# A scheduled GLA loop, one slot deeper, with an order of preference inside the slot

## The chip, the cores and the metric

The kernel runs on one NeuronCore of a Trainium2 chip. The metric is device time in microseconds (us) of one execution, the median of several runs. The engines are TensorE (PE, with its weight loads shown apart as PEld), VectorE (DVE), ScalarE (ACT), GpSimd (POOL) and SyncE (SP, which here only issues DMAs). Each engine takes its instructions in the order in which they stand in its queue.

## What is computed

One inference step of a two-layer backbone over 256 context tokens and 1024 latent tokens, width 1024. Layer 0 mixes tokens by gated linear attention (GLA) in both directions, layer 1 by softmax attention. Both have an adaptive norm in front, a SiLU gate and a residual. The change touches only the GLA layer:

```python
def step(S, inp):                       # per chunk, per head, per direction
    qi, ki, vi, gi = inp
    b = jnp.cumsum(gi, axis=2)
    qe = qi * jnp.exp(b)
    ke = ki * jnp.exp(-b)
    a = jnp.where(mask, jnp.einsum("bhtk,bhsk->bhts", qe, ke), 0.0)
    o = jnp.einsum("bhts,bhsv->bhtv", a, vi) + jnp.einsum("bhtk,bhkv->bhtv", qe, S)
    S = jnp.exp(b_last[:, :, 0, :])[..., None] * S + jnp.einsum(
        "bhsk,bhsv->bhkv", ki * jnp.exp(b_last - b), vi)
    return S, o
...
o = rms_norm(o_f + flip(o_b), onorm).reshape(B, T, GLA_VD).astype(h.dtype)
y = (o * jax.nn.silu(gate)) @ w_out
```

There are 4 heads, with keys of 128 and values of 256 columns. The outputs are both residual streams, the new scan states, and the keys and values of the context.

## The kernel before

Tokens lie in 10 tiles of 128. Products with large weights are made of three float16 products each (high by high, high by low, low by high), eight blocks deep, so one projection is 24 matmuls (`mm3`, line 129).

**The loop.** `gla` runs over heads 0 to 4 and, for each, over the 10 tiles: 50 slots. In a slot of head h it works on two heads at once. For head h it prepares a tile: `decay` makes the log decay (a product into the PSUM bank "z", then absolute value, exp and log on ACT, and a split in two float16 parts on DVE and POOL); `decayed` sums it along the chunk (bank "cs") and scales queries and keys with it (`en`, `qe`); `intra` transposes the scaled keys (bank "kt", line 617), copies them to SBUF (`ks`, DVE, line 619), makes the scores (line 623), masks them with a predicated copy (DVE, line 626) and adds both directions (`at`, POOL, line 628); `outer` makes keys times values (bank "U", lines 639 and 642), copies one direction away (`u`, ACT, line 644) and runs the first scan direction with the other (`Sa` on POOL, `Wa` on DVE, lines 662 and 666); `local` multiplies the scores with the values and the queries with the state into bank "A" (line 682) and ACT copies the result to `oa` (line 684). For head h-1 it finishes a tile: `combine` runs the other scan direction (`Sc`, `Wc`), multiplies it with the queries (bank "o", line 694), adds `oa` and takes the norm; `gated` multiplies with the gate `gx` (DVE, line 706) and writes the product to DRAM (`og_d`, a DMA on SP, line 707). `value_gate` projects values of head h and the gate of head h-1 in one product 512 wide (256 wide in head 0 and in the last pass); ACT takes the halves out of the bank (lines 558 and 562).

Beside these, slots carry pieces of the next head's query and key projections (`qk_piece`, 24 matmuls 512 wide, placed by the table `PIECES`), the conditioning of the next layer (`gemv`, `mod_sum`, `affine`), the loading and splitting of weights (`fill` and `split_ahead`: a maximum on DVE, its power of two over one small matmul in bank "o", `pow2`, then ACT and DVE for the two halves), and at the end the first tiles of the output projection.

**What sets the order.** A scheduler orders each engine's queue while the program is built: it takes the instruction of the lowest priority number that a model of the engines holds ready, and the number grows as the program is written down. In a slot the program is written as: `local` of the slot before, `decayed` of this slot, `decay` two slots ahead, `value_gate` of this slot, `intra`, `combine`, `gated`, fillers, `outer`. The loop has eight PSUM banks: two for "mm" (projections, taken in turn), one each for "z", "cs", "A", "kt", "U" and "o". The scores and the local product share "A". The gate `gx` has two SBUF buffers, `v` two.

Of the kernel before, what the change touches and what calls it, by code (L numbers as in the profile page):

```python
# [43 lines left out]

OUT = (1, 0, 2, 3, 4)

G_SCALE = 32.0
# [6 lines left out]
class K:  # L54
# [22 lines left out]

    def pow2(self, mx, n=1, cross=True):  # L80
# [208 lines left out]
    def gemv(self, l, b, to):  # L289
        nc = self.nc  # L290
        ps = self.bank("mm")
        for k in range(KT):
            j = k % 4
            nc.tensor.matmul(
                ps[32 * j : 32 * j + 32, 0:256], self.cst[:, k, :], to[:, k, :],
                start=k < 4, stop=k >= 4, tile_position=(0, 32 * j), skip_group_check=True,
            )
        m = self.t(self.ew, [P, 256], F32, "mod")
        nc.scalar.copy(m, ps[:, 0:256])
        return l, b, m  # L300
# [43 lines left out]
    def affine_rows(self, gb):  # L344
        ps = self.bank("mm")[0:32, 0:P]
        self.nc.tensor.transpose(ps, gb.rearrange("p s i k -> p (s i k)"), self.ident)
        r = self.t(self.ew, [P, 256], F32, "mod")[0:32, 0:P]
        self.nc.vector.tensor_copy(r, ps)
        self.nc.sync.dma_start(self.gb_d.rearrange("s i (k p) -> (s i k) p", p=P), r)
# [202 lines left out]
    def value_gate(self, h, i, w):  # L552
        a, b = 0 if h < GH else DV, 2 * DV if h > 0 else DV
        ps = self.bank("mm")
        self.tok_proj(i, [t[:, :, a:b] for t in w[0:2]], ps[:, a:b])
        if h < GH:
            v = self.t(self.tl, [P, DV], F32, "v", bufs=2)
            self.nc.scalar.activation(v, ps[:, 0:DV], AF.Copy, scale=self.inv_v[h])
            self.v[h][i] = v
        if h > 0:  # L560
            x = self.t(self.ew, [P, DV], F32, "gx")
            self.nc.scalar.activation(x, ps[:, DV:], AF.Copy, scale=self.inv_g[h - 1])  # L562
            self.silu(x, DV)
            return x
# [7 lines left out]
    def decay(self, h, i):  # L572
        nc = self.nc
        z = self.bank("z")[:, 0 : 2 * DK]
        nc.tensor.matmul(
            z.rearrange("p (d k) -> p d k", d=2), self.r[:, i * P : i * P + P],
            self.wa2[:, :, h * DK : h * DK + DK], start=True, stop=True,
        )
        u = self.t(self.ew, [P, 2 * DK], F32, "ls")
# [5 lines left out]
        nc.vector.scalar_tensor_tensor(g, u, G_SCALE, g, ALU.mult, ALU.add)  # L585
        hi = self.t(self.tl, [P, 2, DK], F16, "ghi", bufs=3)
        lo = self.t(self.tl, [P, 2, DK], F16, "glo", bufs=3)
        hf, lf = (t.rearrange("p d k -> p (d k)") for t in (hi, lo))
# [5 lines left out]
    def decayed(self, h, i, g):  # L594
        nc = self.nc
        cs = self.bank("cs")[:, 0:260].rearrange("p (d k) -> p d k", d=2)
        for d in range(2):
            for j in range(2):
                nc.tensor.matmul(cs[:, d, :], g[j][:, d, :], self.cum[:, d, :], start=j == 0, stop=j == 1)
        en = self.t(self.ew, [P, 2, P], F32, "en")  # L600
# [4 lines left out]
        self.mark = nc.vector.tensor_tensor(en, en, k.unsqueeze(1).to_broadcast([P, 2, P]), ALU.mult).ins  # L605
        qe = self.t(self.tl, [P, 2, P], F32, f"qe{i}")
        nc.vector.tensor_tensor(qe, ep[:, :, 0:P], q.unsqueeze(1).to_broadcast([P, 2, P]), ALU.mult)
        eb = self.t(self.tl, [P, 2, 2], F32, f"eb{i}")
        nc.gpsimd.tensor_copy(eb, ep[:, :, P : P + 2])
        return {"qe": qe, "ke": en, "eb": eb}  # L610

    def intra(self, i, st):
        nc = self.nc
        ke, qe = st["ke"], st["qe"]
        kt = self.bank("kt")[:, 0 : 2 * P].rearrange("p (d k) -> p d k", d=2)
        for d in range(2):
            nc.tensor.transpose(kt[:, d, :], ke[:, d, :], self.ident)
        ks = self.t(self.ew, [P, 2, P], F32, "ks")
        nc.vector.tensor_copy(ks, kt)
        ab = self.bank("A")  # L620
        ap, st["o"] = ab[:, 0 : 2 * P].rearrange("p (d k) -> p d k", d=2), ab[:, 2 * P :]
        for d in range(2):
            nc.tensor.matmul(ap[:, d, :], ke[:, d, :], qe[:, d, :], start=True, stop=True)
        am = self.am[self.ia % len(self.am)]
        self.ia += 1
        nc.vector.copy_predicated(am, self.mask, ap)
        at = self.t(self.tl, [P, P], F32, "at", bufs=2)
        nc.gpsimd.tensor_tensor(at, am[:, 0, :], am[:, 1, :], ALU.add)
        st["at"], st["ks"] = at, ks


    def outer(self, h, i, a, st, prev, last):
        nc = self.nc
        c = 1 - a
        ub = self.bank("U").rearrange("p (d k) -> p d k", d=2)
        v, ks = self.v[h][i], st["ks"]
        needa = i < NTP or not last
        if needa:
            nc.tensor.matmul(ub[:, a, :], ks[:, a, :], v, start=True, stop=True)
        st["u"] = None  # L640
        if i < NTP or prev is not None:
            nc.tensor.matmul(ub[:, c, :], ks[:, c, :], v, start=True, stop=True)
            st["u"] = self.t(self.tl, [P, DV], F32, f"u{i}")
            nc.scalar.copy(st["u"], ub[:, c, :])
        st["S"], st["W"] = self.scan(h, i, a, prev, ub[:, a, :] if needa else None, st["eb"], "a")
# [29 lines left out]
    def local(self, h, i, a, st):  # L675
        nc = self.nc
        o = st["o"]
        terms = [(st["at"], self.v[h][i])]
        if st["S"] is not None:
            terms.append((st["qe"][:, a, :], st["S"]))  # L680
        for j, (x, y) in enumerate(terms):
            nc.tensor.matmul(o, x, y, start=j == 0, stop=j == len(terms) - 1)
        st["oa"] = self.t(self.tl, [P, DV], F32, f"oa{i}")
        nc.scalar.copy(st["oa"], o)


    def combine(self, h, i, c, st, prev):
# [3 lines left out]
        if sc is not None:  # L691
            o = self.bank("o" if h < GH - 1 else ("o", "U", "z", "cs")[self.io % 4])[:, 0:DV]
            self.io += 1
            nc.tensor.matmul(o, st["qe"][:, c, :], sc, start=True, stop=True)
            og = self.t(self.ew, [P, DV], F32, "og", bufs=3)
# [37 lines left out]
    def gla(self, wq, w, filler):  # L733
        asc = list(range(NTP, NT)) + list(range(NTP))
        orders = [asc if h % 2 == 0 else asc[::-1] for h in range(GH + 1)]
        st = [[None] * NT for _ in range(GH)]
        g = {n: self.decay(0, asc[n]) for n in range(2)}
        local = None
        for h in range(GH + 1):
            order = orders[h]  # L740
            a, ends = (0, (NT - 1, NTP - 1)) if h % 2 == 0 else (1, (NTP, 0))
            starts = (NTP, 0) if h % 2 == 0 else (NT - 1, NTP - 1)
            if h < GH:
                self.inv_v[h] = self.mulcol(self.inv_h, w[2][0], self.gcp, f"inv_v{h % 2}")
            if h > 0:
                self.inv_g[h - 1] = self.mulcol(self.inv_h, w[2][1], self.gcp, f"inv_g{h % 2}")
            prev = cprev = None
            for n, i in enumerate(order):
                slot = h * NT + n
                if i in starts:  # L750
                    prev = cprev = None
                if local:
                    self.local(*local)
                    local = None
# [6 lines left out]
                if h < GH:  # L761
# [6 lines left out]
                with self.tc.issue_after(self.mark):  # L768
                    while self.jobs:
                        run(self.jobs.pop(0))  # L770
                filler(slot)
                if h < GH:
                    self.outer(h, i, a, s, prev, i in ends)
                    prev, local = s, (h, i, a, s)
                    if i < NTP and i in ends:
                        self.final_state(h, a, prev)
                if n == 4 and h < GH:
                    nw = self.nw = self.wtile((2, 1)[h % 2])
                    self.jobs.append(self.load_g(nw, h))
# [6 lines left out]
                if h == 1 and n == 3:  # L786
                    self.fold_qk(1, wq)
                if h < GH - 1:
                    for j, c in PIECES[h % 2].get(n, ()):
                        self.qk_piece(h + 1, j, c, wq)  # L790
            if h < GH:
                w = nw

# [514 lines left out]
def emit(ctx, tc, I, O, dbg=None, stop=None):  # L1308
# [29 lines left out]
    with ExitStack() as c:  # L1338
# [285 lines left out]
```

## Time and profile before

| | |
|---|---|
| three timed runs | 1301.16, 1304.89 and 1310.17 us, median 1304.89 |
| the profiled execution | its span from first to last instruction, 1302.5 us |
| PE, DVE, ACT, POOL busy | 1214.8, 923.3, 704.9, 360.3 us |
| mean granted PE clock | 0.983 of full speed |
| GLA loop on the time axis | about 76 to 600 us, the last slots mixed with the output projection |

How to read the profile: busy time is the time in which an engine had an instruction in it; a PE row's duration contains the way through the array, so consecutive matmuls overlap, and what a matmul costs in a stream is the distance between two starts. "Idle before, releaser" is the engine's idle time just before an instruction, and whose result ended it. The granted clock is what the throttle let TensorE have, 1.00 or 0.50 at any moment.

### The profile page before, as it was taken

Reading aid. Unit: us, or ns where it says so; the run is one execution under the profiler, and the core shown is the slowest. Engines: PE = TensorE matmul, PEld = TensorE weight load, DVE = VectorE, ACT = ScalarE, POOL = GpSimd, SP = SyncE. Lnnn points to the kernel's source line nnn. Section 1 sums busy time; section 2 is a strip of 40 time slices with the busy share of each in tenths; the row PEclk is TensorE's granted clock in tenths of the full one; section 3 lists DMA queues with packets and bytes.
Section 4 is the critical chain, followed back from the end, with each engine's and each line's share of the span. In section 5 each row is a group of like instructions: output and inputs, shape, how many; then the busy total and the mean of one; then the engine's idle time right before and its main releaser. Section 6 shows DMA issues by size and latency. Waiting matters only on the chain. (4 is left out here: it accounts for less than half of the span.)

```text
span 1302.5 us, 22246 instructions
## 1 busy us (share of the span) xinstructions
PE 1214.8 (93%) x7936; PEld 783.4 (60%) x7936; DVE 923.3 (71%) x2120; ACT 704.9 (54%) x1706; POOL 360.3 (28%) x594
## 2 busy tenths in 40 slices
PE   4899999999998989896999989999999999989998
PEld 2366666555645556674777657766676667756444
DVE  5575878877876798675776667777667587786652
ACT  3684656565655666541433376666766687673110
POOL 1132214223322143411123334333233344322000
PEclk9899999999998999998999999999999999999999
DMA  9602655554646443269966597676948648879342
GB/s 363 249 33 82 213 156 174 174 158 129 189 141 184 128 146 106 94 158 259 258 147 166 138 209 148 126 138 135 198 94 183 142 90 144 186 138 237 131 148 81
DMA packets 357454, 207.51 MB, mean 159 GB/s; under 512 B 251054, under 2 KB 341438, under 8 KB 354912
## 3 DMA queue, kind: packets, MB, share of 16 engines
q1 hardware_dynamic: 349824, 188.02, 56.4%
q0 software_dynamic: 4080, 12.73, 3.3%
q10 hardware_dynamic: 3440, 5.35, 1.1%
q8 instruction: 62, 1.02, 0.3%
q14 instruction: 48, 0.39, 0.1%
HBM read 107.45 MB, written 37.26 MB: 111 GB/s over the span
## 5 line engine op out<-in xcount | busy, mean ns | idle before, releaser
L129 PEld LDWEIGHTS <-hT_hi 128*128 128x128 f16 x1920 | 189.1, 99 | 122.4 <-issue 7.6
L129 PE MATMUL mm<-whi,hT_hi 128*128 128x512 f16 (+1 forms) x576 | 200.0, 347 | 3.6 <-ACT gx L562 1.9
L129 PE MATMUL mm<-whi,hT_lo 128*128 128x512 f16 (+1 forms) x576 | 199.9, 347 | 0.0
L129 PE MATMUL mm<-wlo,hT_hi 128*128 128x512 f16 (+1 forms) x560 | 193.9, 346 | 0.0
L1139 DVE SCALAR_TENSOR_TENSOR phl<-p,srec,phl 128x1280 f16<-128x1280 f32 (+1 forms) x80 | 108.2, 1355 | 71.7 <-POOL phl L1136 37.0
L129 PEld LDWEIGHTS <-whi 128*128 128x128 f16 x1232 | 120.6, 98 | 60.6 <-issue 2.3
L129 PE MATMUL mm<-hT_hi,whi 128*128 128x256 f16 (+1 forms) x480 | 141.5, 295 | 0.0
L129 PE MATMUL mm<-hT_lo,whi 128*128 128x256 f16 (+1 forms) x480 | 141.3, 294 | 0.0
L129 PE MATMUL mm<-hT_hi,wlo 128*128 128x256 f16 (+1 forms) x480 | 141.3, 294 | 0.0
L129 PEld LDWEIGHTS <-hT_lo 128*128 128x128 f16 x960 | 94.7, 99 | 67.1 <-DMA hT_lo<-k 5.0
L1106 PE MATMUL S<-kT,wst 128*128 128x512 f16 (+1 forms) x624 | 123.5, 341 | 11.5 <-ACT p L1114 10.4
L129 PE MATMUL mm<-PT,vh 128*128 128x256 f16 x672 | 112.2, 273 | 9.7 <-DMA PT<-phl 7.6
L1136 POOL TENSOR_SCALAR phl<-p,srec 128x1280 f16<-128x1280 f32 (+1 forms) x40 | 55.4, 1384 | 192.5 <-DVE srec L1130 78.1
L1109 DVE TENSOR_REDUCE smx<-S 128x1 f32<-128x1280 f32 (+1 forms) x80 | 101.5, 1268 | 9.4 <-PE S L1106 9.1
L1114 ACT ACTIVATE p<-S,snb,sexp 128x1280 f32<-128x1280 f32 (+1 forms) x80 | 99.3, 1242 | 5.3 <-DVE phl L1139 1.8
L1106 PEld LDWEIGHTS <-wst 128*128 128x128 f16 x624 | 61.2, 98 | 65.0 <-issue 13.4
L129 PE MATMUL mm<-PT,vl 128*128 128x256 f16 x336 | 91.6, 273 | 0.0
L152 DVE TENSOR_REDUCE wmx<-wst 128x1 f32<-128x512 f32 x104 | 64.7, 676 | 22.1 <-DMA wst<-in_gla_w_in 8.1
L129 PEld LDWEIGHTS <-wlo 128*128 128x128 f16 x616 | 60.3, 98 | 31.6 <-DVE wlo L1277 1.8
L129 PEld LDWEIGHTS <-vh 128*128 128x128 f16 x672 | 65.1, 98 | 20.6 <-issue 9.2
L944 POOL TENSOR_TENSOR rope<-hx,ropet 128x64 f32<-128x64 f32 x160 | 63.0, 423 | 30.4 <-ACT hx L1070 16.7
L1111 ACT ACTIVATE snb<-smx,nsexp 128x1 f32<-128x1 f32 x80 | 23.3, 291 | 73.6 <-DVE smx L1109 71.6
(370 smaller groups left out, 2712.1 us busy)
## 6 DMA issues: line engine op xcount, KB each, us to landing
wada<-in_w_ada SPq DMA_DIRECT2D x16, 1024.0 KB
wst<-in_gla_w_in SPq DMA_DIRECT2D x12, 1024.0 KB
wst<-in_att_w_in SPq DMA_DIRECT2D x10, 1024.0 KB
og_d<-gx SPq DMA_DIRECT2D x40, 128.0 KB
og_d<-og POOLq DMA_DIRECT2D x40, 128.0 KB, 2.8
wst<-og_d SPq DMA_DIRECT2D x5, 1024.0 KB
xr<-x_d SPq DMA_DIRECT2D x9, 512.0 KB
out<-xr ACTq DMA_DIRECT2D x17, 256.0 KB
```

The lines of the kernel that those rows point to most:

```text
L129: self.pe = self.nc.tensor.matmul(out, a, b, start=k == 0 and j == 0, stop=k == n - 1 and j == 2).ins
L152: nc.vector.tensor_reduce(mx[:, j : j + 1], st[:, 2 * j : 2 * j + 2, :], AX.XY, ALU.max, apply_absolute_value=True)
L944: nc.gpsimd.tensor_tensor(tv[:, h, :, w, :], xv[:, h, :, 1 - w, :], sn[:, :, w, :], ALU.mult)
L1106: nc.tensor.matmul(S[:, a : a + n], x, y, start=m == 0, stop=m == 2)
L1109: last = nc.vector.tensor_reduce(mx, S, AX.X, ALU.max).ins
L1111: nc.scalar.activation(nb, mx, AF.Copy, scale=self.nsexp)
L1114: nc.scalar.activation(p, S, AF.Exp, scale=self.sexp, bias=nb, accum_out=den)
L1136: nc.gpsimd.tensor_scalar(hi, p, r, 2.0 ** 14, ALU.mult, ALU.mult)
L1139: nc.vector.scalar_tensor_tensor(lo, p, r2, hi, ALU.mult, ALU.subtract)
```

## The change

The loop's preparation moves one slot ahead: `decay` three slots ahead instead of two, `decayed` and `value_gate` one slot ahead instead of in the slot itself. `local` stands in its own slot, behind `outer`, instead of at the start of the next. The scores move from bank "A" to the free half of "kt", so that "A" holds the local product alone; `pow2` takes bank "z" instead of "o". `v` gets three buffers, the decays four, `qe` and `eb` become rings of 11 and 12; `mod` drops to one buffer. The key and query pieces move up by about a slot. And each part of a slot gets an offset to its priority from a table: a positive number puts it behind, a negative one ahead.

```diff
+LATER = {
+    "local": 5, "loc": -30, "kt": 30, "A": 10, "intra": -5, "ks": -85,
+    "combine": -15, "cs": -10, "vg": -10, "u": 100, "gated": 60,
+    "decay": -25, "outer": 5, "oa": 220, "Uc": -5, "pieces8": 10,
+}
+    @contextmanager
+    def later(self, name):
+        n = LATER.get(name, 0)
+        self.tc.cur_priority += n
+        yield
+        self.tc.cur_priority -= n
...
-    {4: [(0, 0)], 5: [(1, 0)], 8: [(0, 1)], 9: [(1, 1), (0, 2), (1, 2)]},
-    {4: [(0, 2), (1, 2)], 6: [(0, 1)], 7: [(1, 1)], 9: [(0, 0), (1, 0)]},
+    {3: [(0, 0)], 4: [(1, 0)], 7: [(0, 1)], 8: [(0, 2), (1, 2)], 9: [(1, 1)]},
+    {4: [(0, 2), (1, 2)], 5: [(0, 1)], 6: [(1, 1)], 8: [(0, 0), (1, 0)]},
...
     def intra(self, i, st):
-        kt = self.bank("kt")[:, 0 : 2 * P].rearrange("p (d k) -> p d k", d=2)
+        kt, ap = (
+            t.rearrange("p (d k) -> p d k", d=2)
+            for b in (self.bank("kt"),)
+            for t in (b[:, 0 : 2 * P], b[:, 2 * P :])
+        )
...
     def local(self, h, i, a, st):
-        o = st["o"]
+        o = self.bank("A")[:, 0:DV]
...
                 slot = h * NT + n
-                if local:
-                    self.local(*local)
-                    local = None
                 if h < GH:
-                    s = st[h][i] = self.decayed(h, i, g.pop(slot))
-                h2, n2 = divmod(slot + 2, NT)
-                if h2 < GH:
-                    g[slot + 2] = self.decay(h2, orders[h2][n2])
-                x = self.value_gate(h, i, w)
-                if h < GH:
-                    self.intra(i, s)
+                    s = st[h][i]
+                    with self.later("intra"):
+                        self.intra(i, s)
+                with self.later("decayed"):
+                    ahead_decayed(slot + 1)
+                with self.later("decay"):
+                    ahead_decay(slot + 3)
...
+                with self.later("gate"):
+                    ahead_gate(slot + 1)
                 if h > 0:
-                    og, r, cprev = self.combine(h - 1, i, a, st[h - 1][i], cprev)
-                    self.gated(h - 1, i, og, r, x)
+                    with self.later("combine"):
+                        og, r, cprev = self.combine(h - 1, i, a, old, cprev)
+                    with self.later("gated"):
+                        self.gated(h - 1, i, og, r, x.pop(slot))
...
                 if h < GH:
-                    self.outer(h, i, a, s, prev, i in ends)
-                    prev, local = s, (h, i, a, s)
+                    with self.later("outer"):
+                        self.outer(h, i, a, s, prev, i in ends)
+                    prev = s
+                    with self.later("loc"):
+                        self.local(h, i, a, s)
...
-        k.p2_bank = "o"
+        k.p2_bank = "z"
```

Inside the functions the parts named in the table stand under `later(...)`: the copies `oa` and `u`, the copy `ks` of the transposed keys, the transposes `kt`, the scores `A`, the sums `cs` and others. `ahead_decay`, `ahead_decayed` and `ahead_gate` call `decay`, `decayed` and `value_gate` for a slot number; `ahead_gate` also makes the scales `inv_v` and `inv_g` at the first slot of a head. Three decays, one `decayed` and one gate run ahead of the loop.

More of the change, by code (lines that the diff above doesn't have):

```diff
@@ L45 @@
 OUT = (1, 0, 2, 3, 4)
+LATER = {
+    "local": 5,
+    "loc": -30,
+    "kt": 30,
+    "A": 10,
+    "intra": -5,
+    "ks": -85,
+    "combine": -15,
+    "cs": -10,
+    "vg": -10,
+    "u": 100,
+    "gated": 60,
+    "decay": -25,
+    "outer": 5,
+    "oa": 220,
+    "Uc": -5,
+    "pieces8": 10,
+}
 G_SCALE = 32.0
@@ L574, in decay @@
         z = self.bank("z")[:, 0 : 2 * DK]
[L575 to L578, printed above, removed]
+        with self.later("z"):
+            nc.tensor.matmul(
+                z.rearrange("p (d k) -> p d k", d=2), self.r[:, i * P : i * P + P],
+                self.wa2[:, :, h * DK : h * DK + DK], start=True, stop=True,
+            )
         u = self.t(self.ew, [P, 2 * DK], F32, "ls")
@@ L596, in decayed @@
         cs = self.bank("cs")[:, 0:260].rearrange("p (d k) -> p d k", d=2)
-        for d in range(2):
-            for j in range(2):
-                nc.tensor.matmul(cs[:, d, :], g[j][:, d, :], self.cum[:, d, :], start=j == 0, stop=j == 1)
+        with self.later("cs"):
+            for d in range(2):
+                for j in range(2):
+                    nc.tensor.matmul(cs[:, d, :], g[j][:, d, :], self.cum[:, d, :], start=j == 0, stop=j == 1)
         en = self.t(self.ew, [P, 2, P], F32, "en")
@@ L680, in local @@
             terms.append((st["qe"][:, a, :], st["S"]))
-        for j, (x, y) in enumerate(terms):
-            nc.tensor.matmul(o, x, y, start=j == 0, stop=j == len(terms) - 1)
+        with self.later("local"):
+            for j, (x, y) in enumerate(terms):
+                nc.tensor.matmul(o, x, y, start=j == 0, stop=j == len(terms) - 1)
         st["oa"] = self.t(self.tl, [P, DV], F32, f"oa{i}")
-        nc.scalar.copy(st["oa"], o)
+        with self.later("oa"):
+            nc.scalar.copy(st["oa"], o)
     def combine(self, h, i, c, st, prev):
@@ L693, in combine @@
             self.io += 1
-            nc.tensor.matmul(o, st["qe"][:, c, :], sc, start=True, stop=True)
+            with self.later("o"):
+                nc.tensor.matmul(o, st["qe"][:, c, :], sc, start=True, stop=True)
             og = self.t(self.ew, [P, DV], F32, "og", bufs=3)
@@ L787, in gla @@
                     self.fold_qk(1, wq)
[L788 to L792, printed above, removed]
+                if n != 8:
+                    with self.later("pieces"):
+                        for j, c in pieces:
+                            self.qk_piece(h + 1, j, c, wq)
     def gate_load(self, l):
```

96 lines of the change are left out of this document (65 added, 31 removed).

## The prediction

> **What bounds the kernel now.** I read the page first, then the loop cut into stages, then the waits of PE alone, then the timeline round the longest wait, then the clock.
>
> ```profile
> span 1302.5 us, 22246 instructions
> PE 1214.8 (93%) x7936; PEld 783.4 (60%) x7936; DVE 923.3 (71%) x2120; ACT 704.9 (54%) x1706; POOL 360.3 (28%) x594
> ```
>
> PE is the bound: 93% of the span. The change removes no matmul, so it can only win idle time of PE inside the GLA loop and what that idle time does to the clock. The stages of the loop, with columns length, then busy time (count) of PE, PEld, DVE, ACT, POOL, then granted clock and DMA:
>
> ```profile
> 76.00:193.00 117.00, 114.78 (x857) 79.84 (x857) 86.01 (x222) 66.25 (x158) 30.18 (x57) 1.00 0.42 132
> 193.00:290.00 97.00, 93.92 (x563) 56.04 (x562) 80.33 (x221) 60.70 (x163) 29.84 (x50) 1.00 0.55 172
> 290.00:395.00 105.00, 100.98 (x579) 56.59 (x577) 79.81 (x217) 60.06 (x161) 31.20 (x52) 1.00 0.49 147
> 395.00:480.00 85.00, 83.51 (x457) 47.98 (x458) 64.79 (x173) 50.03 (x128) 24.75 (x36) 0.96 0.51 155
> 480.00:497.00 17.00, 12.25 (x56) 8.38 (x55) 16.21 (x50) 10.13 (x32) 7.69 (x13) 0.80 0.29 97
> 497.00:526.00 29.00, 28.99 (x170) 18.88 (x168) 23.60 (x72) 16.28 (x43) 12.58 (x23) 1.00 0.47 164
> 526.00:556.00 30.00, 23.65 (x163) 17.75 (x162) 19.53 (x53) 18.01 (x51) 11.13 (x18) 0.94 0.25 67
> 556.00:600.00 44.00, 39.48 (x280) 27.34 (x279) 29.99 (x66) 18.04 (x39) 6.81 (x12) 0.96 0.74 170
> ```
>
> Length minus PE's busy time is PE's idle time: 2.2 us in head 0 (76 to 193), 3.1 + 4.0 + 1.5 = 8.6 in heads 1 to 3 (193 to 480), 4.75 in 480 to 497, none to 526, 6.35 in 526 to 556 and 4.5 after that. Who ended it (engine, line, waited for, us in total, times, longest):
>
> ```profile
> PE A L682 <- POOL at L628: 7.1, 5, 3.8
> PE y L129 <- DMA hT_lo<-k: 4.5, 1, 4.5
> PE U L639 <- DVE ks L619: 2.0, 1, 2.0
> PE mm L129 <- ACT gx L562: 1.9, 1, 1.9
> PE o L694 <- DVE p2m L92: 1.7, 1, 1.7
> PE kt L617 <- DVE en L605: 1.1, 1, 1.1
> ```
>
> The largest item is `local` (L682) waiting for the masked scores `at`. The 4.5 us of the output projection wait for transposing DMAs behind the loop, which the change does not touch; that leaves 2.2 + 8.6 + 4.75 + 6.35 = 21.9 us. How the longest wait comes about:
>
> ```profile
> 390.75 0.71 PE L623 MATMUL A<-qe,en 128*128 128x128 f32 x4
> 392.02 1.33 ACT L209 ACTIVATE split<-wst,p2s 128x512 f16<-128x512 f32 x2 [2.81 <-DMA w_o<-split]
> 392.77 0.75 DVE L210 SCALAR_TENSOR_TENSOR split<-wst,p2s,split 128x512 f16<-128x512 f32 x1 [2.15 <-ACT split L209]
> 395.04 0.44 DVE L626 COPY_PREDICATED am<-mask,A 128x256 f32<-128x256 int32 x1
> 395.56 0.87 POOL L628 TENSOR_TENSOR at<-am 128x128 f32<-128x128 f32 x1 [5.39 <-DVE am L626]
> 396.49 1.22 PE L682 MATMUL A<-v,at 128*128 128x256 f32 x2 [3.82 <-POOL at L628]
> ```
>
> The scores start at 390.75. The masking copy needs 0.44 us, but stands in DVE's queue behind the weight split L210, which waits for ACT's split L209, which waited 2.81 us for a DMA to free its buffer. So the scores' way to `local` took 5.7 us, and PE had only a `gemv` and one small product to put between. It is no slow operation; it is a queue that is late now and then, and too little PE work between a producer and its consumer.
>
> The clock follows. Four stretches of 3.41 us, three of them just ahead of a cut, and then the three cuts, in the columns of the stages:
>
> ```profile
> 391.41:394.82 3.41, 1.26 (x16) 0.47 (x15) 2.05 (x6) 2.53 (x4) 0.00 (x0) 1.00 0.27 83
> 480.15:483.57 3.42, 1.98 (x14) 1.36 (x13) 3.42 (x11) 3.13 (x11) 2.59 (x5) 1.00 0.35 101
> 483.57:486.98 3.41, 1.07 (x7) 0.84 (x7) 3.41 (x10) 1.43 (x6) 0.59 (x2) 1.00 0.83 283
> 538.19:541.60 3.41, 1.68 (x8) 0.84 (x6) 2.60 (x10) 1.41 (x7) 2.99 (x6) 1.00 0.12 38
> 394.82:401.65 6.83, 5.16 (x12) 3.28 (x13) 4.65 (x9) 5.55 (x16) 1.06 (x2) 0.50 1.01 315
> 486.98:493.81 6.83, 6.04 (x19) 4.15 (x18) 6.04 (x22) 4.45 (x13) 3.62 (x5) 0.50 0.12 41
> 541.60:545.01 3.41, 3.41 (x13) 1.96 (x12) 1.34 (x5) 3.28 (x12) 1.63 (x3) 0.50 0.62 190
> ```
>
> Each stretch at 0.50 follows one in which PE was busy 37, 31 or 49%; after the stretch at 58% nothing was cut. At half clock half of the busy time is lost: 2.6, 3.0 and 1.7 us, 7.3 together. So the ceiling of this change is 21.9 + 7.3 = 29 us, 2.2% of the span.
>
> **The change part by part.** What the scheduler made of the priorities can be counted in PE's queue of both programs. I price what stands between two instructions by distances of starts:
>
> ```profile
> 299.63 0.59 PE L682 MATMUL A<-v,at 128*128 128x256 f32 x2
> 300.06 0.59 PE L682 MATMUL A<-Sa,qe 128*128 128x256 f32 x2
> 300.49 0.38 PE L129 MATMUL mm<-whi,hT_hi 128*128 128x512 f16 x1
> 300.71 0.38 PE L129 MATMUL mm<-wlo,hT_hi 128*128 128x512 f16 x1
> 519.77 0.27 PE L129 MATMUL mm<-wlo,hT_hi 128*128 128x256 f16 x1
> 519.88 0.27 PE L129 MATMUL mm<-whi,hT_lo 128*128 128x256 f16 x1
> ```
>
> Two rows of a 256-wide float32 product take 0.43, a 512-wide float16 matmul 0.22 and a 256-wide one 0.11; a projection of 24 is then 5.2 us, in head 0 and the last pass 2.6.
>
> *Scores to local.* Before, between the scores and `local` lie 0.6 to 9.1 us of PE work (estimates by those prices), under 3 us in 16 of 40 tiles and under 1 us in four. After, with `local` behind the projection of its own slot, it is 5.2 us or more in 27 tiles and under 3 us in two. The delay of 5.7 us above would be covered but for a few tenths. The usual way, 0.44 + 0.87 us, is covered everywhere.
>
> *Keys to outer.* `ks`, at -85 first in DVE's order, had under 1.5 us between its transposes and `outer` in 13 tiles; after, in two. This takes the 2.0 us of L639 except there.
>
> *`pow2` in "z" instead of "o".* `combine` then no longer waits for DVE to read the maximum (1.7 us). Now the next decay product can wait for it instead; in the new queue 1.3 to 6 us of PE work lie between the two, and `decay` is three slots early, so I cost it at nothing; without that cover it is the same 1.7.
>
> *Decay sums and `en` one slot ahead.* The median distance from sums to transposes stays 7.2 us; the waits of 1.1 on `en` fell in the crowded stretch below. No gain counted.
>
> *Sharing of "kt" by transposes and scores.* The next transposes now wait for the masking copy as well as for `ks`. Their distance has a median of 6.9 us and falls to 1.1 once, in head 0. *The freed "A"*: the scores no longer wait for ACT's copy `oa`, which at +220 moves behind other ACT work; `local` of the next tile has 7 us to wait for it.
>
> *What stays.* Two stretches are no better in the new queue. In 480 to 497 the projection stands behind the transposed scales of the next layer, which take an "mm" bank in turn; there two tiles' small products still follow each other with nothing large between (0.5 us from transposes to `outer`, 1.4 from sums to transposes). In the last pass three groups of two to four `combine` products stand together, and each waits for the state scan. Head 0 even gains a crowded spot: tiles 4 and 5 follow each other without a projection (0.7 and 1.1 us), which the old queue had less tightly.
>
> *SP and ACT.* The write of `gx` at +60 goes later into SP's queue, and loads behind it wait with it; they are asked for slots ahead, so nothing. But `value_gate` a slot earlier refills a `gx` buffer a slot earlier, with still two of them: a new wait, behind which `v`, `en` and the copies queue on ACT. It is the second rival.
>
> **The sum**, each term the idle and clock time of its stage times what I expect to go: heads 1 to 3, 8.6 + 2.6 = 11.2, of which 10 go (ends 4 and 11.2; near the upper, as the two longest waits are exactly those that get 5.2 us of cover). 480 to 497, 4.75 + 3.0 = 7.75, of which 3 go (0 to 7.75; it stays crowded). 526 to 556, 6.35 + 1.7 = 8.0, of which 4 go (0 to 8; the 1.9 us on `gx` and some of the `combine` waits). Head 0: 1 us worse (2.5 worse to 2 better). Together 10 + 3 + 4 - 1 = 16 us. The span becomes 1302.5 - 16 = 1286.5. The three runs have a median of 1304.89, 2.4 above the profiled span, which I add: 1288.9.
>
> The Trainium skill ("TensorE: Matmul & The Clock Gate", "HAM oscillation") says that the clock is halved after idle gaps of more than about 3.4 us. This trace does not agree: in 483.57 to 486.98 no gap was longer than 2.0 us and PE was busy 31%, and the clock was cut. By the page's rule no stage of the new order would lose clock, as no wait that I expect reaches that length: all 7.3 us would be won in place of the 4.7 in my sum, and the time would be 1286. I go by the rows.
>
> **The rivals.** *The waits move.* DVE and ACT still run the same splits in the same loop, and those are held by DMAs as at 392.02; the new queues put other consumers behind them, and the crowded stretches lose what the middle wins. For it: DVE is busy 80 of 97 us in head 1, so a late item pushes all behind it. Against it: the cover has grown in nearly every tile. If 5 of the 11.2 go and head 0 and the last stretches lose 3, the time is 1304.9 - 2 = 1303.
>
> *The gate's buffers.*
>
> ```profile
> L562 ACT ACTIVATE gx<-mm,inv_g 128x256 f32<-128x256 f32 x40 | 18.6, 465 | 11.1 <-PE mm L129 7.7 <-DMA og_d<-gx 3.4
> og_d<-og POOLq DMA_DIRECT2D x40, 128.0 KB, 2.8
> ```
>
> ACT already waited 3.4 us for a write of `gx` to land. With the projection one slot ahead and `gated` put back, the write of tile s-1 must land before the projection of tile s+1 is taken out. Landing took 2.8 us for a like write in layer 1. In heads 1 to 3 a slot has 5.2 us of projection and more, and this hides. In the last pass it has 2.6, and PE stops when gating, write and landing take longer than two projections, 5.2 us. At 8 us for each of the 10 tiles the loss is 10 x 2.8 = 28 us, against 13 won before it (10 + 3 + 1 for the stretch, less 1): 1304.9 + 15 = 1320. Against it: the wait was seen twice in 40.
>
> *It does not do what it says*: the queues show that it does; the time would be 1305.
>
> **How the numbers follow.** Forecast 0.58, with a range of its own of 1275 (the ceiling of 29) to 1299; the waits move 0.24; the gate's buffers 0.16; no effect 0.02. The range reaches from 1274 over the second case to 1308, and leaves out the third case and little else. A measurement of this kernel tells about 1% from no change, 13 us. Faster by more: nine tenths of the forecast, 0.53. Slower by more (over 1318): most of the third case, with a few worse cases of the second, 0.14. The rest, 0.33, is within 1%.
>
> **What would show it.** The wait of `local` for `at` should fall from 7.1 to under 2 us, that of `outer` for `ks` to under 1.5; PE's idle time between 193 and 480 from 8.6 to about 1, with no half-clock stretch there; 480 to 497 should still show one. Wrong would be: idle time on `kt` or "z" in heads 1 to 3, ACT's wait for the `gx` write above 10 us, or a loop that ends early while the next stage then waits for DMAs longer than 4.5 us.

## The result, and the profile after

The changed kernel takes 1292.32 us, the median of nine runs (1288.11 to 1300.83), against 1304.89 us for the kernel before in nine runs beside it (1299.87 to 1310.17): a ratio of 0.9907, with a 95% interval of 0.9885 to 0.9929. The head of the profile page after, its span and then the busy time of each engine:

```profile
span 1291.9 us, 22221 instructions
PE 1209.2 (94%) x7936; PEld 778.7 (60%) x7936; DVE 920.0 (71%) x2120; ACT 706.0 (55%) x1706; POOL 353.3 (27%) x594
```

The span is 10.6 us shorter. The stages of the loop, in the columns of the prediction (length, then busy time and count of PE, PEld, DVE, ACT, POOL, granted clock, DMA share, GB/s). The loop now runs ahead of the old one (the scores that started at 482.57 start at 463.28), so heads 1 to 3 end at 450 here; the next two rows keep the prediction's bounds, 193 to 480 and 480 to 497. The last three rows are stretches round the two half-clock periods that the changed loop has:

```profile
193.00:450.00 257.00, 256.60 (x1499) 147.07 (x1491) 204.53 (x560) 158.21 (x413) 70.77 (x124) 1.00 0.55 169
450.00:526.00 76.00, 69.77 (x391) 44.01 (x384) 66.74 (x192) 48.72 (x131) 29.17 (x47) 0.96 0.41 132
526.00:556.00 30.00, 24.91 (x178) 18.05 (x176) 21.16 (x61) 17.09 (x49) 13.04 (x23) 1.00 0.35 95
193.00:480.00 287.00, 282.54 (x1624) 161.54 (x1617) 229.41 (x628) 174.41 (x457) 82.75 (x142) 0.99 0.53 162
480.00:497.00 17.00, 15.16 (x84) 9.88 (x82) 16.70 (x52) 11.37 (x36) 8.16 (x14) 1.00 0.43 140
463.69:467.10 3.41, 1.61 (x12) 1.08 (x9) 3.41 (x10) 0.66 (x2) 0.68 (x2) 1.00 0.00 0
467.10:470.51 3.41, 3.41 (x9) 1.18 (x9) 3.17 (x16) 2.57 (x9) 2.83 (x4) 0.50 0.23 78
494.41:497.82 3.41, 1.57 (x9) 1.07 (x7) 3.41 (x13) 0.58 (x3) 1.48 (x4) 1.00 0.11 38
```

Heads 1 to 3 (193 to 450) are full: 0.4 us of idle time, no half clock. The stretch after them (450 to 526) is idle for 6.2 us, and two cuts of the clock, 3.41 us each and full of work, cost half of that each. Who ended PE's idle time in the loop (engine, line, waited for, us in total, times, longest):

```profile
PE y L155 <- DMA hT_lo<-k: 4.9, 1, 4.9
PE U L676 <- DVE ks L658: 2.2, 2, 1.8
PE mm L155 <- ACT gx L589: 1.8, 4, 0.6
PE o L736 <- POOL Sc L701: 1.6, 1, 1.6
PE A L722 <- POOL Sa L699: 1.4, 1, 1.4
PE z L736 <- POOL Sc L701: 1.4, 1, 1.4
PE z L604 <- DVE p2m L118: 1.3, 1, 1.3
```

No row has `local` waiting for `at` any more (7.1 us before); the 1.4 us of L722 are a wait for the scan state `Sa`. Two milestones that both kernels have show the rest: the first projection in the setup, and the first and last matmul of the output projection `y`. First the kernel before, then the changed one, in the view of groups (line, engine, operation, count, duration in ns min/median/max, first to last start):

```profile
L531 PE MATMUL mm<-hT_hi,whi x32: 379/379/631, 44.8 to 73.4; 128*128 128x512 f16 x32
...
L129 PE MATMUL y<-whi,hT_hi x128: 272/326/634, 582.7 to 732.8; 128*128 128x512 f16 x64, 128*128 128x256 f16 x64
```

```profile
L557 PE MATMUL mm<-hT_hi,whi x32: 379/379/631, 47.4 to 76.1; 128*128 128x512 f16 x32
...
L155 PE MATMUL y<-whi,hT_hi x128: 272/326/634, 574.3 to 720.3; 128*128 128x512 f16 x64, 128*128 128x256 f16 x64
```

So the first projection comes 2.6 us later. From there to the first `y` it is 526.9 us instead of 537.9, 11.0 less, and from the first `y` to the end 717.6 instead of 719.8, 2.2 less: 2.6 - 11.0 - 2.2 = -10.6. The loss ahead of the loop is in the setup. Rows of PE's timeline there (start, us, operation, and in brackets the idle time before it with its releaser):

```profile
27.44 1.11 PE L420 MATMUL z<-ident,x 128*128 128x128 f32 x4 [2.28 <-DVE xT L1458]
29.33 1.11 PE L420 MATMUL z<-ident,x 128*128 128x128 f32 x4 [0.79 <-DVE xT L1458]
31.23 0.27 PE L113 MATMUL z<-ident,wm 128*128 128x128 bf16 x1 [0.78 <-DVE xT L1458]
```

The first tiles' transposes use bank "z" too, and `pow2` (L113), which the change moved there for the whole stage and not for the loop alone, now stands in line with them.

### The profile page after: what moved, and what is told of

Read it like the earlier page. It is cut to its first block, busy times and chain, and to the rows that moved or that the text cites. A ratio compares the mean times of both kernels' runs of the same rounds, so it can differ in the third digit from the quotient of the medians.

```text
span 1291.9 us, 22221 instructions
## 1 busy us (share of the span) xinstructions
PE 1209.2 (94%) x7936; PEld 778.7 (60%) x7936; DVE 920.0 (71%) x2120; ACT 706.0 (55%) x1706; POOL 353.3 (27%) x594
```

## The experiments

Two theories stood at first. *Cover*: the depth and the slot order put a projection between each small product and its consumer, and that is the gain. *Preference*: the offsets decide it. Twelve kernels ran. The table gives for each the ratio to the kernel before, and from one profiled execution the start of the first projection, the time from there to the first `y` ("loop"), from the first `y` to the end ("behind"), and what PE loses in 193 to 450: idle time plus half of its busy time at half clock.

| kernel | ratio [95%] | first projection | loop | behind | lost, heads 1-3 |
|---|---|---|---|---|---|
| before | 1 | 44.8 | 537.9 | 719.8 | 11.2 |
| changed | 0.9907 [0.9885, 0.9929] | 47.4 | 526.9 | 717.6 | 0.4 |
| e1 | 0.9926 [0.9899, 0.9954] | 47.2 | 525.8 | 719.1 | 1.1 |
| e2 | 0.9889 [0.9863, 0.9915] | 45.1 | 527.7 | 718.0 | 0.9 |
| e3 | 0.9964 [0.9944, 0.9983] | 47.1 | 527.2 | 726.1 | 0.8 |
| e4 | 1.0044 [1.0027, 1.0061] | 45.3 | 530.7 | 730.9 | 3.9 |
| e5 | 1.0016 [0.9998, 1.0035] | 44.6 | 536.5 | 722.0 | 5.8 |
| e6 | 1.0016 [0.9992, 1.0040] | 45.7 | 534.0 | 728.8 | 2.5 |
| e7 | 0.9905 [0.9878, 0.9932] | 44.6 | 528.3 | 718.0 | 2.8 |
| e8 | 0.9965 [0.9941, 0.9989] | 45.9 | 523.3 | 727.4 | 0.6 |
| e9 | 1.0052 [1.0031, 1.0073] | 44.7 | 534.7 | 729.1 | 1.1 |
| e10 | 0.9973 [0.9954, 0.9992] | 45.4 | 523.6 | 726.1 | 0.7 |
| e11 | 1.0045 [1.0020, 1.0070] | 44.9 | 536.7 | 729.1 | 6.2 |
| e12 | 0.9934 [0.9905, 0.9963] | 45.2 | 529.5 | 723.3 | 0.9 |

How far one profiled execution may be trusted can be read from kernels with the same slot order, offsets and banks in the loop: changed, e1 and e2 have 525.8 to 527.7; e3, e10 and e12 have 523.6 to 529.5; e5 and e11 differ by 0.2, e6 and e9 by 0.7. So loops that are alike differ by up to 5.9 us, and a smaller difference between two loops is not read from one execution each. The first projection is steadier: 44.6 to 45.9 and 47.1 to 47.4 us over all fourteen kernels.

**e1_ref**: the changed kernel once more, as the reference for e2 to e4 on their chip.

> The changed kernel again, on the same chip as the next three, as their reference. Expected as measured first: 1292 us, a ratio of 0.988 to 0.993, PE idle 0.4 us between 190 and 450, and half clock near 467 and 498.

The time repeats: 1296.08 us against 1305.56 before. The half-clock periods of the loop do not: e1 has one, at 532.03, where two were expected near 467 and 498, and heads 1 to 3 lose 1.1 us instead of 0.4.

**e2_setup_bank**: `pow2` goes back to bank "o" in the setup and takes "z" only in the loop.

```diff
-        k.p2_bank = "z"
+        k.p2_bank = "o"
...
+        k.p2_bank = "z"
         k.gla(wq, wv, filler)
```

> The changed kernel with the power-of-two products back in bank o ahead of the loop and in bank z only inside it. The queues differ from the changed kernel's only ahead of the loop. If the 2.6 us by which the first projection starts later (47.42 against 44.82) come from these products sharing z with the transposes of the first tiles, the first projection starts at about 44.8 again and the time falls by 2 to 3 us, to a ratio of about 0.988. If the late start is the DMAs' or chance, it stays at 47.4 and the time with it.

1292.09 us beside e1's 1296.08 on the same chip, 4.0 less, though the intervals of the two ratios overlap. The group of the first projection in e2:

```profile
L557 PE MATMUL mm<-hT_hi,whi x32: 379/379/634, 45.1 to 73.7; 128*128 128x512 f16 x32
```

It starts 2.1 us earlier than in e1 (47.2). In the table the kernels with "o" in the setup start it at 44.6 to 45.9, the three with "z" (changed, e1, e3) at 47.1 to 47.4. So the loss ahead of the loop is the setup's sharing of "z". e2 has the lowest ratio of all kernels here.

**e3_flat**: the change with every offset at zero.

```diff
-LATER = {
-    "local": 5,
...
-    "pieces8": 10,
-}
+LATER = {}
```

> The changed kernel with every offset of the order of preference at zero: the deeper loop alone. Cover theory: the scores' distance to the local product has a median of 6.3 us in its queue (5.5 with the offsets), so nearly all of the win stays: ratio 0.989 to 0.995, PE idle under 2 us in heads 1 to 3. Preference theory: the offsets make the win, and without them the ratio is 0.997 or more, with waits on the masked scores and on the copied keys back.

**e4_pref**: the kernel before in depth, order and banks, with the offsets of the same table round the same parts.

```diff
...
                 if local:
-                    self.local(*local)
+                    with self.later("loc"):
+                        self.local(*local)
...
```

> The kernel before with the same offsets on the same parts, its loop not deeper and its banks as they were. Cover theory: the distance from scores to local product is under 3 us in 11 of 40 tiles (16 before, 2 after), so less than half of the win comes: ratio 0.995 to 1.003, waits of the local product on the masked scores still above 2 us. Preference theory: most of the win, 0.990 to 0.994.

The ratios fit neither theory: 0.9964 lies between the two for e3, and e4 is slower than before. The stages tell more. In heads 1 to 3 the change without offsets loses 0.8 us, and its loop takes 527.2, as short as with them. The offsets alone leave 3.9 us there and take the loop to 530.7, 7.2 of the 11.0 us. So the deeper loop does not need the offsets, but most of the loop's gain can be had without the deeper loop. What differs is a stage that neither edit touches: behind the first `y`, e3 takes 726.1 us and e4 730.9, the changed kernel 717.6. In e4 it is one wait of PE, in the view of its waits:

```profile
PE y L155 <- DMA hT_hi<-oghl: 13.4, 1, 13.4
```

**e5_bank_o**: `pow2` in bank "o" in the loop as well. **e6_share_a**: e2 with the scores back in bank "A" beside the local product.

```diff
-        k.p2_bank = "z"
+        k.p2_bank = "o"
```

> The changed kernel with pow2's small product in bank "o" all through, as before the change; it differs from e2_setup_bank (ratio 0.9889, bank "o" in the setup, "z" in the loop) in the loop alone, so it prices the step that I costed at nothing. My step: the next decay product has enough cover, so the bank decides nothing in the loop; ratio within 0.002 of e2's, the wait of z on p2m (1.0 us in e2) goes and a wait of o on p2m of at most 1.7 us comes. Rival: the wait of z sits in the crowded stretch, where every us ends up in the time; ratio 0.987 to 0.988 and a span 1 to 2 us shorter than e2's 1290.8.

```diff
-        kt, ap = (
...
-        )
+        kt = self.bank("kt")[:, 0 : 2 * P].rearrange("p (d k) -> p d k", d=2)
+        ab = self.bank("A")
+        ap, st["o"] = ab[:, 0 : 2 * P].rearrange("p (d k) -> p d k", d=2), ab[:, 2 * P :]
...
-        o = self.bank("A")[:, 0:DV]
+        o = st["o"]
```

> e2_setup_bank with the scores back in bank "A" beside the local product, as before the change; the slot order, the depth and the offsets stay. Theory (the depth and the order give the cover, the bank only follows): heads 1 to 3 (193 to 450 us) keep 2 us or less of idle time, the wait of local for at stays under 1.5 us, ratio 0.989 within 0.002. Rival (the freed bank gives the cover, because scores and local of one tile no longer wait for the local product and the copy of the tile before): the queue puts local under 3 us behind the scores in 6 of 40 tiles instead of 2, the waits for at come back with 3 to 5 us and one half-clock stretch with them, ratio 0.992 to 0.995.

Both lose the whole gain, more than any theory had. With "o" the loop takes 536.5 us (e11, the same loop, 536.7) against e2's 527.7: nearly all of the 11.0 is gone. In heads 1 to 3 `local` waits again, but not for `at`: 1.9 us for `v` and 1.6 for ACT's copy `oa`. ACT's timeline of e5 at one of them, and the two rows of PE and DVE that hang on it:

```profile
245.75 0.41 ACT L266 ACTIVATE ls<-ls 128x256 f32<-128x256 f32 x1
249.26 1.33 ACT L235 ACTIVATE split<-wst,p2s 128x512 f16<-128x512 f32 x2 [3.09 <-DMA w_g<-split]
250.02 0.75 DVE L236 SCALAR_TENSOR_TENSOR split<-wst,p2s,split 128x512 f16<-128x512 f32 x1 [1.84 <-ACT split L235]
250.50 0.45 ACT L585 ACTIVATE v<-mm,inv_v 128x256 f32<-128x256 f32 x1
251.10 1.19 PE L722 MATMUL A<-v,at 128*128 128x256 f32 x2 [1.94 <-ACT v L585]
```

It begins like the chain of 392.02 in the prediction: ACT stands at a split whose buffer a DMA still holds. Here it is `v` that stands behind the split. With the scores in "A" (e6, e9) heads 1 to 3 lose only 2.5 and 1.1 us, but the loop takes 534.0 and 534.7, 6 to 9 more than in changed, e1 and e2. That is little over the spread of like loops, but both executions show it: idle and clock time from 450 to the first `y` are 18.5 and 20.5 us against e2's 14.4. So the deeper loop gives its gain only with both banks moved.

**e7_split3**: the kernel before, with the tile of the weight split in halves, and three of them.

```diff
-        for i in range(2):
-            a = slice(i * h, i * h + h)
-            t = self.t(self.spl, [P, 2, h, 256], F16, "split")
...
+        for i in range(4):
+            a = slice(2 * i, 2 * i + 2)
+            t = self.t(self.spl, [P, 2, 2, 256], F16, "split", bufs=3)
...
```

> The kernel before, with the weight split's tile in halves and three of them in place of one, so that a split need not wait for the DMA that reads the last one. Theory (the masked scores are late because DVE stands behind a split whose buffer a DMA still holds): the wait of local for at falls from 7.1 us to under 3, heads 1 to 3 lose under 5 us to idle time and clock instead of 11.2, ratio 0.994 to 0.997. Rival (the scores are late because DVE is busy with long instructions of any kind, and only PE work between scores and local helps): the wait for at stays at 5 us or more, ratio 0.998 to 1.003.

The ratio is 0.9905, better than the theory's own range and level with the change, from an edit that leaves the slots, the banks and the offsets as they were. PE's waits in its loop:

```profile
PE mm L129 <- ACT gx L560: 4.8, 3, 2.5
PE mm L129 <- DVE s L318: 2.3, 1, 2.3
PE A L680 <- POOL at L626: 2.2, 4, 1.2
```

`local` waits 2.2 us for `at` instead of 7.1, as the theory had it. But its cause is not shown. ACT's waits for the DMAs that hold the split's buffer, 193 to 600 us, before and then in e7:

```profile
ACT split L209 <- DMA w_g<-split: 5.3, 4, 2.4
ACT split L209 <- DMA w_o<-split: 2.8, 1, 2.8
ACT split L209 <- DMA w_q<-split: 1.4, 2, 0.7
```

```profile
ACT split L207 <- DMA w_g<-split: 6.0, 4, 2.7
ACT split L207 <- DMA w_o<-split: 1.9, 1, 1.9
ACT split L207 <- DMA w_q<-split: 1.1, 2, 0.8
```

That is 9.5 us and 9.0: the waits stayed. The scores are only a little less late: from the end of the scores to the end of `at` it is over 3 us in 11 of the 40 tiles, 10 before, and at most 6.0 us, 7.8 before (worked out from the rows of PE and POOL). And the order on PE came out another way. The tile that cost 3.82 us before, with its scores at 390.75, had 1.2 us of PE work between them and `local`; in e7 its scores are at 385.33, `at` is done 3.1 us after them instead of 5.0, and 6.2 us of work stand between, a projection with them. So e7 reaches the same time, and how much of that is the smaller tile and how much the new order on PE is open. The two changes together were not tried.

**e8_gx3**: e2 with three gate buffers, paid for with two `og` buffers instead of three.

```diff
-            x = self.t(self.ew, [P, DV], F32, "gx")
+            x = self.t(self.ew, [P, DV], F32, "gx", bufs=3)
...
-            og = self.t(self.ew, [P, DV], F32, "og", bufs=3)
+            og = self.t(self.ew, [P, DV], F32, "og", bufs=2)
```

> e2_setup_bank with three gate buffers instead of two, paid for with two og buffers instead of three. The second rival of the prediction said that the write of gx to DRAM holds the gate's buffers and ACT with them; ACT's wait for it did grow from 3.4 to 6.0 us in the changed kernel, and PE waited 1.6 to 1.8 us for gx. If that wait is on the path: ACT's wait for og_d falls under 1.5 us, PE's waits for gx under 0.5, ratio 0.987 to 0.988. If it is beside the path (PE waits for gx because ACT is behind with other work): ACT's wait falls all the same, PE's waits for gx stay over 1 us, ratio within 0.0015 of e2's 0.9889.

The group in which ACT takes the gate out of the bank, in the changed kernel and then in e8 (after the bar busy us, mean ns, then idle time before it with its releasers):

```profile
L589 ACT ACTIVATE gx<-mm,inv_g 128x256 f32<-128x256 f32 x40 | 18.6, 466 | 11.4 <-DMA og_d<-gx 6.0 <-PE mm L155 5.3
```

```profile
L589 ACT ACTIVATE gx<-mm,inv_g 128x256 f32<-128x256 f32 x40 | 18.7, 467 | 7.7 <-PE mm L155 5.5 <-DMA og_d<-gx 1.9
```

The wait falls to 1.9 us, PE's waits for `gx` to 0.5, and the loop is 523.3 us, 4.4 less than e2's, which one execution does not tell apart (e10, with two gate buffers, has 523.6). But behind the loop it takes 727.4, and the ratio is 0.9965. As a version it loses; about the loop it says that the gate's buffers cost at most some 4 us.

By now one thing separated the good ratios from the bad: behind the first `y`, before, changed, e1, e2 and e7 take 717.6 to 719.8 us, all others 722.0 to 730.9. In e3, e5, e6 and e8, PE's queue has 36 to 41 more matmuls of `y` ahead of the first key tile `kv`, and PE stood at them, in e6 for 14.4 us. So the next three held the third 72 matmuls of `y` behind the key tile, where before and the changed kernel have them.

```diff
-            last = self.residual(i, lambda k: (hT[:, k, :], lT[:, k, :]), wo, inv, x)
+            with self.tc.issue_after(self.pe) if n == n0 + 2 else ExitStack():
+                last = self.residual(i, lambda k: (hT[:, k, :], lT[:, k, :]), wo, inv, x)
```

**e9_share_a_pin**, **e10_flat_pin** and **e11_bank_o_pin** are e6, e3 and e5 with that (e10 with "o" in the setup, too).

> e6_share_a again (scores and local product in one bank), but with one thing held behind the loop: the third 72 matmuls of the output projection stand behind the first key tile on PE, as they do in the kernel before and in the changed one. In e6 36 of them stood ahead of it and PE waited 14.4 us there for the transposes of the last tiles. Theory (e6 lost its gain to that order behind the loop, and the bank costs what heads 1 to 3 show, 2.5 us of idle time against 0.9): the wait of 14.4 falls to under 6, last y under 726 us, ratio 0.990 to 0.994. Rival (the shared bank itself spoils the time): ratio 0.997 or more.

> The changed kernel with all offsets at zero, pow2 in bank "o" in the setup, and the third 72 matmuls of the output projection held behind the first key tile, where they stand in the kernel before. Theory (the depth gives the gain, the offsets nothing that lasts; e3_flat's smaller gain was the order behind the loop, 12.8 us of waits there): ratio as in e2_setup_bank, 0.987 to 0.991. Rival (the order of preference inside the slot is needed in the last pass, where e3 lost 5.6 us to the state scan on POOL): ratio 0.993 to 0.997.

> e5_bank_o again (pow2 in bank "o" all through), with the same order held behind the loop. It differs from e2_setup_bank in the bank of pow2 inside the loop alone. Theory (the bank costs little in the loop, e5 lost 15.5 us to the order behind it): heads 1 to 3 still lose 4 to 6 us as in e5 (0.9 in e2), the rest returns; ratio 0.991 to 0.994, so that bank "z" in the loop is worth 2 to 5 us. Rival (the bank is worth nothing, e5's loss in heads 1 to 3 was a side effect too): ratio 0.987 to 0.990. Second rival (the bank is worth the whole gain): 0.997 or more.

The theory missed in all three: nothing was won back. The rivals' numbers hold for e9 and e11, and e10 lies just above its rival's, though not for that rival's reason, as its loop takes 523.6 us and is not long in the last pass. PE now stands at `kv` instead of at `y`, as long as before. In e10, in the view of PE's waits:

```profile
PE kv L96 <- DVE amx L1060: 17.9, 1, 17.9
```

So PE's order is not the cause; the late thing is further back. SP's timeline of e2 there (start, us that the issue took, DMA), and then that of e10:

```profile
583.62 0.49 SPq L749 DMA_DIRECT2D og_d<-gx  x1
584.22 2.86 SPq L403 DMA_TRANSPOSE hT_hi<-split  x1
587.17 2.14 SPq L403 DMA_TRANSPOSE hT_lo<-split  x1
...
591.64 0.43 SPq L978 DMA_DIRECT2D wkv<-w_kv  x1
592.12 1.41 SPq L979 DMA_DIRECT2D wkv<-w_kv  x1
593.57 3.95 SPq L936 DMA_DIRECT2D xr<-in_x_sample  x1
```

```profile
579.56 5.61 SPq L962 DMA_DIRECT2D wkv<-w_kv  x1
585.21 3.13 SPq L963 DMA_DIRECT2D wkv<-w_kv  x1
588.38 3.27 SPq L919 DMA_DIRECT2D xr<-in_x_sample  x1
591.75 0.38 SPq L732 DMA_DIRECT2D og_d<-gx  x1
592.23 1.66 SPq L386 DMA_TRANSPOSE hT_hi<-split  x1
593.98 2.69 SPq L386 DMA_TRANSPOSE hT_lo<-split  x1
```

In e10 the weight loads of the next stage stand on SP ahead of the last gate write and the transposes of the last early tile. In before, changed, e1, e2, e4 and e7 they stand behind both; in e3, e5, e6 and e8 to e11 ahead of the transposes. In e6 the two loads took only 0.43 us each there, and behind the first `y` it took 728.8 us all the same.

**e12_flat_sp**: e10 with the loads `wkv` (the pair with `j` = 1 below) and `xr` held behind those transposes; `tr` is the last of them.

```diff
...
+                    with self.tc.issue_after(tr) if j else ExitStack():
-                    nc.sync.dma_start(hi, d[:, 0, :, b])
-                    nc.sync.dma_start(lo, d[:, 1, :, b])
+                        nc.sync.dma_start(hi, d[:, 0, :, b])
+                        nc.sync.dma_start(lo, d[:, 1, :, b])
```

> e10_flat_pin (depth alone, no offsets) with one more thing held behind the loop: the loads wkv and the residual rows xr stand on SP behind the transposes of the last early tile (hT from split), as in the kernel before and in e2_setup_bank. In e10 they stood ahead: SP spent 5.61, 3.13 and 3.27 us on issuing them from 579.6 on, the split that the transposes read was written by 582.6, the transposes were issued at 592.2, and PE waited 17.9 us at the first key tile. Theory (the order on SP behind the loop decides whether what the loop wins is kept): PE's wait there falls to 5 to 9 us, what is lost between the first and the last y from 20.3 to 12 to 14 us, ratio 0.989 to 0.992. Rival (the wait has another source and moves on to the next DMA or to DVE): the loss there stays at 17 us or more, ratio 0.996 or more.

The ratio comes down from 0.9973 to 0.9934, between the two theories and with intervals that overlap. "Behind" falls from 726.1 to 723.3, and what PE loses between the first and the last `y` from 20.3 to 17.2 us, the rival's number. PE's wait is shorter, but far from the theory's 5 to 9 us:

```profile
PE kv L96 <- DVE amx L1063: 15.0, 1, 15.0
```

SP's order is at most a part of it. The other part is not settled: e4 has the good order on SP and still waited 13.4 us.

## Why the prediction was right, point by point

The forecast of 1288.9 us stands 3.4 us from the median, and the direction and the mechanism of its main term hold: cover for late scores. The size is in part luck. On the span it forecast 16 us and 10.6 came. The stages from 76 to 556 gave 11.4 of the 16. The setup's 2.6 us and the 2.2 us behind the loop, neither of them in the sum, nearly cancel. And the prediction added 2.4 us from span to median, where the changed kernel has 0.4: that alone brings the forecast 2 us nearer.

- *Heads 1 to 3*, 10 of 11.2 us to go: 10.8 went up to 450 (11.2 to 0.4), and the wait of `local` for `at` fell from 7.1 to none. It is the cover and not sooner scores: in the changed kernel the way from the scores to `at` is over 3 us in 18 of 40 tiles (10 before), ACT's splits wait 15.3 us for DMAs in 193 to 450 (9.5 before), and PE does not feel it. e3, e10 and e12 show that the offsets are not needed for it. But the prediction's bounds were 193 to 480, and it foresaw about 1 us of idle time and no half clock in them; there are 4.5 us and the half-clock period of 467.10. It did not reckon that the crowded stretch would move ahead with the loop: the tile whose scores started at 482.57 now has them at 463.28. By its own bounds 5.0 of the 11.2 went, and 5.9 of 7.75 in 480 to 497; the terms below are told apart by the work, at 450.
- *480 to 497 and 526 to 556*, 3 + 4 = 7 us to go: about 1 went. From 450 to 526 the changed kernel loses 6.2 us idle and 3.4 to the clock, 9.6, against 4.75 + 3.0 = 7.75 before, so 1.9 worse where 3 better was forecast. From 526 to 556 it loses 5.1 instead of 8.0, so 2.9 of 8.0 and not 4. This is the term that was mis-sized: the prediction saw that the stretch stays crowded and still gave it a gain. `outer` waits for `ks` 1.8 us there, 2.2 in all, over the 1.5 that it set as a limit.
- *`pow2` in "z", at nothing*: wrong twice. In the setup it costs 2.6 us, which the prediction did not look at, as it followed the bank into the loop alone. In the loop the next decay product does wait for it, 1.3 us, and this is the largest gap in the stretch ahead of the half clock at 467.10. But left in "o" (e5, e11) it costs the loop 9 us. *The freed "A"*, counted without a term: with the scores back in it (e6, e9) the loop loses 6 us or more. Both banks were costed as waits of one product, and not as freedom for the whole queue.
- *Head 0*, 1 us worse: PE's idle time in 76 to 193 is 2.6 us, 2.2 before, so 0.4 worse.
- *The wait behind the loop that the change does not touch*: `y` for its transposes, 4.5 and now 4.9, just over the 4.5 that the prediction set as a mark. The stage behind the loop is not untouched: it gave 2.2 us here, and in nine of the experiments it was 2 to 11 us longer than before.
- *The gate's buffers*: the wait came, 3.4 to 6.0 us on ACT, under the 10 that were set as its mark. PE's share of it is 1.8 us in the changed kernel. The rival's 28 us in the last pass did not come.
- *The waits move*: in 450 to 526 they did, by the 1.9 us above, on `ks`, `p2m` and the scans on POOL.
- *The offsets* had no term of their own. In the deeper loop they have no effect that can be read (changed, e1, e2 against e3, e10, e12: a mean of 526.8 each). The kernels with them are faster all the same (e2's 0.9889 against 0.9973 and 0.9934), behind the loop, where no offset stands.
- *The clock*: the two cuts of the changed loop came after stretches in which PE was busy 1.61 and 1.57 of 3.41 us, 47 and 46%. The largest gaps in them, worked out from PE's rows, were 1.35 and 1.84 us. So they bear out the prediction's reading against the rule on gaps over 3.4 us. The Trainium skill ("TensorE: Matmul & The Clock Gate", "A second HAM failure mode: psum-queue depth-cycling") also tells of frequent short idle times between groups of matmuls that make the clock swing; with that the trace agrees. The busy share alone does not tell when a cut comes, as the last section shows.

What stays open: why the stage behind the loop is 2 to 11 us longer in e3 to e6 and e8 to e12; of that e12 shows at most some 3 us as SP's order, in intervals that overlap. Why e5's loop needs bank "z": that `local` then waits for ACT is shown, but not how the bank moves it. And by what e7 wins.

The lowest ratio here is e2's, 0.9889 at 1292.09 us; its interval overlaps those of the changed kernel and of e7.

## What to carry to other kernels

Before a pipeline is made deeper to hide a late result, try a small edit at the head of the late queue: here a few lines that cut the split's tile gave the same 0.99 as the whole change. Then look in the trace whether the edit did what it was made for: the waits that it was to end were still there. Where a scheduler orders the queues, compare kernels by milestones and not by their times alone: edits in the loop moved a later stage by as much as the whole change was worth, and few of the twelve ratios can be read without that. When a helper changes its bank, follow it through every stage that calls it.

## What the runs showed of the hardware

In each trace here the cuts of the loop start a whole number of stretches of 3.41 us apart (before: 394.82, 486.98 and 541.60, which are 27 and 16 of them), so the stretch that ends at a cut can be read. The clock was cut with PE busy about half and only short gaps: in e2 a stretch at 46% ended in a cut at 531.35 with no gap over 0.96 us. But the share of one stretch does not decide. In the kernel before, one at 58% (from 480.16) was not followed by a cut, nor was one at 45% (from 548.42), while in e4 one at 52% was (cut at 239.91). The changed kernel and e1 are one program, and PE is busy 1.57 us in the stretch from 494.4 in both: the first was cut at 497.82, the second was not.

The same DMA takes very different times to issue on SP: the two `wkv` loads 0.43 and 1.41 us in e2, 5.61 and 3.13 in e10, where they stand straight behind `xr` and `wlo`; a transpose took 10.20 us before (590.27). What sets it is not shown. The next issue on SP came only after it in each case, so on SP the place of a transfer can count for more than its own 0.4 us.
